# Decoder trunk on one core: attention's third unit turned by a DMA transpose that GpSimd lays out, the second unit's value products placed inside a weight product

## The chip, the cores and the metric

The kernel runs on one core of a Trainium2 chip. The engines are PE (TensorE: matmuls and transposes), DVE (VectorE), ACT (ScalarE), POOL (GpSimd) and SP (SyncE, which here issues DMAs). Each works through its own instructions in order, and semaphores connect them. The metric is the device time of one execution in microseconds (us).

## The reference

The reference is a trunk of two layers on 512 tokens with 1024 features. Each layer is half a gated feed-forward block, a mixer, and a second half feed-forward block:

```
for l in range(DEPTH):                                  # 2
    x = x + 0.5 * swiglu(rms_norm(x, n1), wg1, wu1, wd1)     # D_FF 2816
    h = rms_norm(x, mix_norm[l])
    z = h @ w_in[l]      # q 512 | k 128 | v 128 | conv_B 512 | conv_C 512 | conv_h 512
    attn = sliding_window_attention(q, k, v, attn_sink[l])
    conv = conv_B * depthwise_causal_conv3(conv_C * conv_h)
    x = x + concat([attn, conv]) @ w_out[l]
    x = x + 0.5 * swiglu(rms_norm(x, n2), wg2, wu2, wd2)
return rms_norm(x, final_norm)

# attention: 8 query heads of 64, 2 key/value heads, blocks of 128 tokens,
# each block sees itself and the block before it (window 128)
scores = q @ k_band / 8 + alibi_bias
m = max(max(scores), sink)
p = exp(scores - m) / (sum(exp(scores - m)) + exp(sink - m))
out = p @ v_band
```

All inputs and outputs are float32.

## The kernel before

Matmuls run in a rounded 32-bit format, so every operand is split into a high part (a cast) and a low part (what the cast left). A product of two split operands is three matmuls: high by high, low by high, high by low. Weights are loaded by DMA as `raw`, ACT casts `wh_n` (line 228), DVE subtracts `wl_n` (line 228 too). The number n counts weight slices through the whole program. A slice is split some products ahead of its use: `need_split` issues the split, and `tc.issue_after` pins it behind a given instruction.

The feed-forward blocks use a seven-product scheme (line 842 holds its matmuls). The mixer's input projection `w_in` is worked as 18 slices of 128 output columns. One `product()` of a slice is 24 matmuls over 512 tokens: eight values of k, and for each the three at lines 318 (xh, wh), 319 (xl, wh) and 321 (xh, wl). The first matmul that reads `wl_n` is thus the third of its product.

Attention is cut into eight `Unit(n, g)`, four token blocks by two key/value heads. Units 0 to 3 are the blocks of head group 0, and 4 to 7 those of group 1. In names, `o_0_1_0` is layer 0, block 1, group 0, so unit 1; the third unit is unit 2, `_0_2_0`. A unit has these stages:

- scores: eight matmuls into PSUM tiles `sc` (lines 1554 and 1555). DVE adds the bias and takes maxima, one scan (line 1558, shown as ISA or CUSTOM_DVE_ANT_0) and one accumulator read for each of four heads. It negates the maxima (`nm`, line 1569). ACT takes four exponentials (1575) and that of the sink (`es`, 1578). DVE adds, inverts and scales `p` (1579 to 1583).
- turn: `p` is transposed to have keys on partitions. Units that aren't in `SEND_AT` are turned by PE: per half of the keys four 128x128 transposes into `pt` (1616). ACT then casts `ph` from it (1621), and DVE subtracts `pl` (1622).
- send and join, for the units in `SEND_AT`: ACT copies `p`, as pairs of 16-bit words, into a spare tile `crossing` with the halves of the words apart (1590, 128x2048 u16). SP issues a DMA transpose from there back into `p` (1592). When the unit is to be turned, ACT puts the halves together again (join, 1601, two copies) and `ph` and `pl` come from that.
- values: four matmuls `o` (two for the first block), of `ph` and `pl` with the values `vv` (1633, 1634). ACT copies half of it out (`ol`, 1636), and DVE adds the halves into `mixed[0]` (1639).

The mixer runs in steps. After each `product()` (slices 114 to 125) `go_on()` calls `attend(step)`, from step 6 on. That issues, in this order, the send due at this step, then the values, the turn and the scores of the units whose entries in `VALUES_AT`, `TURN_AT` and `SCORES_AT` are this step. Then `go_on` asks for the next split, pinned behind the last instruction that `attend` returned. The step that is a product's own can put a stage inside it: `INSIDE = (11, 4, 5)` puts unit 4's turn ahead of k = 5 in the product of step 11, which is slice 119. Around the change, step 8 follows product 116, step 9 product 117, step 10 product 118 and step 11 product 119. The order of the code is kept on PE; on DVE and ACT a scheduler orders what the code issues by what it can start when.

Beside attention the same steps run the convolution: DVE multiplies `ch` (1707), ACT makes `cc` and `tap` (1709, 1711), DVE adds the third tap into `tap` (1712), GpSimd adds and multiplies `cc` (1715, 1716).

`mixed` is two tiles of 128x4x512. `mixed[0]` takes attention's output. `mixed[1]` takes the convolution's: columns 0 and 1 after products 118 and 119, columns 2 and 3 after products 124 and 125.

Of the kernel before, what the change touches and what calls it, by code (L numbers as in the profile page):

```python
# [54 lines left out]
STREAM_BACK_AT = {9: 0, 11: 1, 16: 2, 18: 3}  # L55
SCORES_AT = (5, 6, 7, 8, 9, 10, 12, 13)

SEND_AT = {7: 1, 9: 3, 11: 5}
TURN_AT = (6, 9, 8, 11, 10, 13, 14, 15)
VALUES_AT = (7, 10, 9, 12, 11, 14, 15, 16)  # L60
INSIDE = (11, 4, 5)
WARM = 3
XT_TAGS = ("sc", "aux", "aux", "mm", "sc", "sc", "aux", "aux")

# [11 lines left out]
def trunk_kernel(  # L76
# [23 lines left out]
    nc = tc.nc  # L100
# [8 lines left out]
    def psum(tag, shape, name):  # L109
        return ps.tile(shape, F32, tag=tag, bufs={"mm": 4, "sc": 2, "aux": 2}[tag], name=name)  # L110

    def g2(name, dt=F32, shape=(P, S)):
        return work.tile(list(shape), dt, tag="g2", bufs=14, name=name)

    def g8(name, dt=F32R, shape=(P, 2, 2, S)):
        return work.tile(list(shape), dt, tag="g8", bufs=4, name=name)
# [15 lines left out]
    def f32(ap):  # L132
        return ap.bitcast(F32)

    def words(ap):

        return ap.bitcast(U16).rearrange("p (n two) -> p two n", two=2)
# [164 lines left out]
    def take_split(ahead=SPLIT_AHEAD):  # L302
        n = state["group"]
        state["group"] += 1
        need_split(n + ahead)
        return n, *split_of.pop(n)

    def group(rhs, between=None, own=None, order=range(KC), tag="mm"):

        n, hi, lo = own or take_split()  # L310
        acc = psum(tag, [P, S], f"acc_{n}")
        order = order[: len(rhs)]
        first, last = order[0], order[-1]
        late = n == OPEN
        for k in order:
            if between:
                between(k, hi, lo)
            nc.tensor.matmul(acc, hi[:, k, :], rhs[k][0], start=k == first, stop=False)  # L318
            nc.tensor.matmul(acc, hi[:, k, :], rhs[k][1], start=False, stop=False)  # L319
            if not late:  # L320
                nc.tensor.matmul(acc, lo[:, k, :], rhs[k][0], start=False, stop=k == last)  # L321
        if late:
            for k in order:
                nc.tensor.matmul(acc, lo[:, k, :], rhs[k][0], start=False, stop=k == last)
        return acc
# [1168 lines left out]
    def mix(l, norm, after):  # L1494
        q = [None] * NH

        mixed = [g8(f"m_{l}_{j}", F32, (P, KC // 2, S)) for j in range(2)]
# [37 lines left out]
        class Unit:  # L1535
# [49 lines left out]
            def send(self):  # L1585


                self.room = crossing[:, todo.index(self) // 2 % 2, :]
                halves = self.room.bitcast(U16).rearrange("p (two n) -> p two n", two=2)
                nc.scalar.copy(halves, words(self.p.rearrange("p h k -> p (h k)")))  # L1590
                self.turned = self.p.rearrange("p h k -> p (h k)").bitcast(U16)
                nc.sync.dma_start_transpose(
                    self.turned.rearrange("p (c q) -> p c q", q=P),
                    halves.rearrange("p two n -> p (two n)"),
                )
# [11 lines left out]
            def turn(self):  # L1607

                self.pt = []
                for kb in range(self.lo // P, 2):  # L1610
                    if todo.index(self) in SEND_AT.values():
                        tp = self.join(kb)
                    else:
                        tp = psum("aux", [P, 4, P], f"pt_{self.name}_{kb}")
                        for h in range(4):
                            nc.tensor.transpose(
                                tp[:, h, :], self.p[:, h, kb * P : (kb + 1) * P], ident
                            )
                    hi = g2(f"ph_{self.name}_{kb}", F32R, (P, 4, P))
                    lo = g2(f"pl_{self.name}_{kb}", F32R, (P, 4, P))  # L1620
                    nc.scalar.copy(hi, tp)
                    last = nc.vector.tensor_sub(lo, tp, f32(hi))
                    self.pt.append((kb, hi, lo))
                return last

# [17 lines left out]
        todo = [Unit(n, g) for g in range(NKV) for n in range(NT)]  # L1643
        crossing = g8(f"crossing_{l}", F32, (P, 2, 4 * 2 * P))

        def attend(step):

            done = None
            if step in SEND_AT:
                todo[SEND_AT[step]].send()  # L1650
            for at, stage in ((VALUES_AT, "values"), (TURN_AT, "turn"), (SCORES_AT, "scores")):
                if stage == "turn" and step + 1 == INSIDE[0]:
                    done = todo[VALUES_AT.index(step)].added
                    continue
                if step in at:
                    done = getattr(todo[at.index(step)], stage)() or done
            return done

        for j in range(NH // 2):
            acc = group(norm.h) if j else qacc  # L1660
            if j == 3:
                vv = take_values()
            qf = scaled(acc, f"qf_{l}_{j}", by=1.0 / 8.0)
            both = form(f"q_{l}_{j}", shape=(P, 2, S))
            qe, qo = both[:, 0, :], both[:, 1, :]
            nc.scalar.copy(qe[:HD, :], qf[:HD, :])
            nc.scalar.copy(qo[HD:, :], qf[HD:, :])
            nc.vector.tensor_sub(qe[HD:, :], qf[:HD, :], f32(qe[:HD, :]))
            nc.vector.tensor_sub(qo[:HD, :], qf[HD:, :], f32(qo[HD:, :]))
            q[2 * j], q[2 * j + 1] = qe, qo  # L1670
            attend(2 + j)
# [4 lines left out]
        step = 6  # L1676

        def product():

            def between(k, hi, lo):  # L1680
                if step == INSIDE[0] and k == INSIDE[2]:
                    todo[INSIDE[1]].turn()

            return group(norm.h, between, own=take_split(SPLIT_AHEAD - 1))

        def go_on():

            nonlocal step
            last = attend(step)
            if step == TURN_AT[-1]:  # L1690
                state["turned"] = last.ins
            step += 1
            with tc.issue_after(last.ins) if last else nullcontext():
                need_split(state["group"] - 1 + SPLIT_AHEAD + (step >= TURN_AT[-1]))

        for pair in range(2):
            cs = []
            for j in range(2):
                c = g2(f"cc_{l}_{pair}_{j}")
# [4 lines left out]
            for j in range(2):  # L1704
                c = 2 * pair + j
# [13 lines left out]
            for j in range(2):  # L1719
                last = nc.vector.tensor_mul(mixed[1][:, 2 * pair + j, :], product(), ys[j])  # L1720
# [64 lines left out]
```

## Time and profile before

| | |
|---|---|
| time, median of 3 runs | 1626.1 us (1625.88 to 1626.62) |
| profiled execution: its time | 1626.19 us |
| profiled execution: its span | 1624.4 us |
| granted TensorE clock | 0.999 |
| PE busy | 1615.4 us, 99% |
| DVE busy | 1376.7 us, 85% |
| ACT busy | 1178.1 us, 73% |
| POOL busy | 216.5 us, 13% |
| layer 0's attention steps | about 368 to 450 us of the span |
| layer 1's attention steps | about 1171 to 1252 us of the span |

The span runs from the first to the last instruction of the profiled execution; its time holds 1.8 us more. In rows of the timeline the first number is the start in us from the span's start, the second the duration; a suffix x4 says that four like instructions stand in one row. Names there have their numbers left out (`wl` for `wl_119`), so the place in time says which one it is. Matmuls overlap: the start of the next tells more than a duration.

### The profile page before, as it was taken

To read this page: it belongs to the slowest core of one execution; us is meant where nothing else is said; L and a number is where in the kernel's file an instruction comes from. 1 tells how busy PE (TensorE), PEld (TensorE's weight loads), DVE (VectorE), ACT (ScalarE), POOL (GpSimd) and SP (SyncE) were. 2 spreads that over 40 slices of the span, in tenths; PEclk is the share of its full clock that TensorE was granted. 3 is DMA by queue.
4 is the path that set the end of the run, shared out by engine and by line. 5 is a ranking of instruction groups with operands and counts; after the bars stand their busy time and mean duration, and the time that the engine had idled before them with its cause. 6 is when DMAs were issued, how large, how long until landed. Compare 5 with 4: busy or idle time off the path is not lost.

```text
span 1624.4 us, 21158 instructions
## 1 busy us (share of the span) xinstructions
PE 1615.4 (99%) x7571; PEld 1349.4 (83%) x7571; DVE 1376.7 (85%) x1788; ACT 1178.1 (73%) x1511; POOL 216.5 (13%) x191
## 2 busy tenths in 40 slices
PE   9999999999999999999999999999999999999998
PEld 7888888888898888888888888888888988888887
DVE  7978798988899977798998777989688998678997
ACT  6677777857766677778866777788586767878665
POOL 1211111001211111111011111110012111111121
PEclk9999999999999999999999999999999999999999
DMA  9999989822597698999767999998136978999892
GB/s 270 212 232 209 220 207 226 233 59 78 143 227 175 177 225 214 218 214 225 218 144 182 224 215 226 215 221 217 42 91 156 233 149 219 225 223 222 241 230 72
DMA packets 306031, 313.92 MB, mean 193 GB/s; under 512 B 125501, under 2 KB 188549, under 8 KB 305925
## 3 DMA queue, kind: packets, MB, share of 16 engines
q1 hardware_dynamic: 265412, 230.90, 50.1%
q0 software_dynamic: 40048, 81.27, 29.3%
q8 instruction: 59, 0.97, 0.2%
q14 instruction: 48, 0.39, 0.1%
q10 hardware_dynamic: 464, 0.40, 0.1%
HBM read 264.29 MB, written 2.10 MB: 164 GB/s over the span
## 4 chain that ended last, share of the span: by engine, by line
PE 98%; DVE 1%; DMA 0%; SPq 0%; issue 0%; ACT 0%; DVEq 0%
PE x L842 27%; PE y L842 13%; PE x_s L842 9%; PE acc L318 7%; PE acc L319 7%; PE acc L321 7%; PE w L842 7%; PE y_s L842 5%; PE x_m L827 3%; PE w_s L842 3%; PE y_m L827 1%; PE y_e L842 1%; PE acc L699 1%; PE x_e L842 1%; PE w_m L827 1%; PE sc L1555 0%
## 5 line engine op out<-in xcount | busy, mean ns | idle before, releaser
L228 DVE TENSOR_TENSOR wl<-raw,wh 128x1024 fp32r<-128x1024 f32 (+1 forms) x494 | 598.6, 1219 | 162.8 <-ACT wh L228 161.9
L228 ACT CAST wh<-raw 128x1024 fp32r<-128x1024 f32 (+1 forms) x494 | 514.1, 1044 | 304.6 <-PE x L842 92.8
L318 PE MATMUL acc<-xh,wh 128*128 128x512 f32 x392 | 153.3, 393 | 0.5 <-ACT wh L228 0.5
L319 PE MATMUL acc<-xl,wh 128*128 128x512 f32 x392 | 153.1, 391 | 0.0
L321 PE MATMUL acc<-xh,wl 128*128 128x512 f32 x384 | 149.7, 390 | 0.0
L223 POOL DMA_DIRECT2D raw<-in_ffn_wu_dram x40 | 50.6, 1272 | 381.6 <-DMA raw<-in_ffn_wu_dram 268.6
L318 PEld LDWEIGHTS acc<-xh,wh 128*128 128x128 f32 x392 | 73.8, 188 | 15.0 <-ACT wh L228 0.6
L319 PEld LDWEIGHTS acc<-xl,wh 128*128 128x128 f32 x392 | 73.7, 188 | 14.5
L321 PEld LDWEIGHTS acc<-xh,wl 128*128 128x128 f32 x384 | 72.1, 188 | 15.3
L223 POOL DMA_DIRECT2D raw<-in_ffn_wd_dram x34 | 41.0, 1218 | 272.0 <-DMA raw<-in_ffn_wd_dram 122.3
L223 POOL DMA_DIRECT2D raw<-in_ffn_wg_dram x40 | 49.1, 1237 | 201.9 <-DMA raw<-in_ffn_wu_dram 84.7
L269 DVE TENSOR_TENSOR raw<-raw,raw 128x1024 f32<-128x1024 f32 x58 | 70.5, 1220 | 1.7 <-DMA raw<-in_ffn_wu_dram 1.2
L1106 ACT COPY raw_a<-turned 128x1024 uint16<-128x1024 uint16 x48 | 63.5, 1357 | 0.0
L842 PE MATMUL x<-wl,ft1h 128*128 128x512 f32 x160 | 62.4, 390 | 0.0
L842 PE MATMUL w<-wh,fb21h 128*128 128x512 f32 x160 | 62.3, 390 | 0.0
L842 PE MATMUL y<-wh,ft3h 128*128 128x512 f32 x160 | 62.3, 390 | 0.0
L842 PE MATMUL x<-wh,ft1l 128*128 128x512 f32 x160 | 62.3, 389 | 0.0
L842 PE MATMUL x<-wl,ft2h 128*128 128x512 f32 x160 | 62.3, 389 | 0.0
L842 PE MATMUL x<-wh,ft2l 128*128 128x512 f32 x160 | 62.3, 389 | 0.0
L842 PE MATMUL x<-wh,ft1h 128*128 128x512 f32 x160 | 62.3, 389 | 0.0
L842 PE MATMUL w<-wh,fb21l 128*128 128x512 f32 x160 | 62.2, 389 | 0.0
L842 PE MATMUL y<-wh,ft3l 128*128 128x512 f32 x160 | 62.2, 389 | 0.0
(517 smaller groups left out, 4545.2 us busy)
## 6 DMA issues: line engine op xcount, KB each, us to landing
raw<-in_ffn_wu_dram SPq DMA_DIRECT2D x127, 512.0 KB, 5.6
raw<-in_ffn_wd_dram SPq DMA_DIRECT2D x105, 512.0 KB, 5.6
raw<-in_ffn_wg_dram SPq DMA_DIRECT2D x86, 512.0 KB, 5.3
raw<-in_ffn_wu_dram POOLq DMA_DIRECT2D x40, 512.0 KB, 9.1
raw<-in_ffn_wg_dram POOLq DMA_DIRECT2D x40, 512.0 KB, 6.5
raw<-in_w_in_dram SPq DMA_DIRECT2D x36, 512.0 KB, 4.0
raw<-in_ffn_wd_dram POOLq DMA_DIRECT2D x34, 512.0 KB, 8.2
raw<-in_w_out_dram SPq DMA_DIRECT2D x20, 512.0 KB, 4.6
```

The lines of the kernel that those rows point to most:

```text
L223: nc.gpsimd.dma_start(out=r, in_=rows_of(*more), accum_op=ALU.add)
L228: return nc.scalar.copy(hi, raw), eng.tensor_sub(lo, raw, f32(hi))
L269: nc.vector.tensor_add(a11, a11, s1)
L318: nc.tensor.matmul(acc, hi[:, k, :], rhs[k][0], start=k == first, stop=False)
L319: nc.tensor.matmul(acc, hi[:, k, :], rhs[k][1], start=False, stop=False)
L321: nc.tensor.matmul(acc, lo[:, k, :], rhs[k][0], start=False, stop=k == last)
L699: nc.tensor.matmul(opening[n], (lo if part == "w" else hi)[:, k, :], xl if part == "x" else xh, start=n not in begun, stop=k == KC - 1 and ...
L827: nc.tensor.matmul(accs[c // 2][:, c % 2, :], w[:, k, cols], x_[:, 2 * h + k, :], start=start and c % 2 == 0 and h + k + i == 0, stop=h + ...
L842: nc.tensor.matmul(accs[u], x_[:, 2 * h + k, tok], w[:, k, :], start=start and h + k + i == 0, stop=h + k == 2 and i == 2, skip_group_chec ...
L1106: nc.scalar.copy(words(raws[self.b][:, c, :]), self.to[:, :, c, :])
```

## The change

Unit 2 is sent at step 8. GpSimd makes the copy that lays the words apart, and it goes not to `crossing` but to columns 2 and 3 of `mixed[1]`, which are written only after product 124. Unit 2 is turned at step 10 (before: 8) and its values stand at step 11, after product 119 (before: 9, after product 117). Unit 1's values, at step 10 before, now stand inside product 119, ahead of k = 3. Unit 4's turn stays inside that product ahead of k = 5. What the next split is pinned to at step 10 is the last subtraction `pl` of unit 1 (`parted`), where it was the last addition into `mixed[0]`.

```diff
-SEND_AT = {7: 1, 9: 3, 11: 5}
-TURN_AT = (6, 9, 8, 11, 10, 13, 14, 15)
-VALUES_AT = (7, 10, 9, 12, 11, 14, 15, 16)
-INSIDE = (11, 4, 5)
+SEND_AT = {7: 1, 8: 2, 9: 3, 11: 5}
+TURN_AT = (6, 9, 10, 11, 10, 13, 14, 15)
+VALUES_AT = (7, None, 11, 12, 11, 14, 15, 16)
+INSIDE = {(11, 3): (1, "values"), (11, 5): (4, "turn")}
+IDLE_LAYS = (2,)
...
             def send(self):
-                self.room = crossing[:, todo.index(self) // 2 % 2, :]
+                n = todo.index(self)
+                self.room = crossing[:, n // 2 % 2, :]
+                if n == 2:
+                    self.room = mixed[1][:, 2:4, :].rearrange("p c s -> p (c s)")
                 halves = self.room.bitcast(U16).rearrange("p (two n) -> p two n", two=2)
-                nc.scalar.copy(halves, words(self.p.rearrange("p h k -> p (h k)")))
+                whole = words(self.p.rearrange("p h k -> p (h k)"))
+                (nc.gpsimd.tensor_copy if n in IDLE_LAYS else nc.scalar.copy)(halves, whole)
...
-                    last = nc.vector.tensor_sub(lo, tp, f32(hi))
+                    last = self.parted = nc.vector.tensor_sub(lo, tp, f32(hi))
...
             for at, stage in ((VALUES_AT, "values"), (TURN_AT, "turn"), (SCORES_AT, "scores")):
-                if stage == "turn" and step + 1 == INSIDE[0]:
-                    done = todo[VALUES_AT.index(step)].added
-                    continue
-                if step in at:
-                    done = getattr(todo[at.index(step)], stage)() or done
+                for n in (n for n, when in enumerate(at) if when == step):
+                    if (n, stage) in INSIDE.values():
+                        done = todo[1].parted
+                    else:
+                        done = getattr(todo[n], stage)() or done
...
             def between(k, hi, lo):
-                if step == INSIDE[0] and k == INSIDE[2]:
-                    todo[INSIDE[1]].turn()
+                if (step, k) in INSIDE:
+                    n, stage = INSIDE[step, k]
+                    getattr(todo[n], stage)()
```

In the rows of order that follow, numbers behind the last underscore only tell tiles apart, and lines of the changed kernel are one to six higher. All rows are layer 0's; layer 1 has the same.

PE, from the end of product 118 (`acc_118`) into product 119, before: unit 1's four value matmuls, unit 5's eight score matmuls (`sc_0_1_1`), then the product.

```order
L321 MATMUL acc_118_3575<-xh_1_6_2840,wl_118_3480 128x512
L1633 MATMUL o_0_1_0_3601<-ph_0_1_0_0_3528,vv_0_3202 128x512
L1634 MATMUL o_0_1_0_3601<-pl_0_1_0_0_3529,vv_0_3202 128x512
L1633 MATMUL o_0_1_0_3601<-ph_0_1_0_1_3533,vv_0_3202 128x512
L1634 MATMUL o_0_1_0_3601<-pl_0_1_0_1_3534,vv_0_3202 128x512
L1554 MATMUL sc_0_1_1_0_3612<-kh_0_3070,q_0_2_3159 128x256
...
L1555 MATMUL sc_0_1_1_1_3619<-kl_0_3071,q_0_3_3207 128x256
L318 MATMUL acc_119_3648<-xh_1_0_2886,wh_119_3571 128x512
L319 MATMUL acc_119_3648<-xl_1_0_2887,wh_119_3571 128x512
L321 MATMUL acc_119_3648<-xh_1_0_2886,wl_119_3572 128x512
```

The same place in the changed kernel:

```order
L322 MATMUL acc_118_3550<-xh_1_6_2840,wl_118_3464 128x512
L1555 MATMUL sc_0_1_1_0_3588<-kh_0_3070,q_0_2_3159 128x256
...
L319 MATMUL acc_119_3624<-xh_1_0_2886,wh_119_3546 128x512
L320 MATMUL acc_119_3624<-xl_1_0_2887,wh_119_3546 128x512
L322 MATMUL acc_119_3624<-xh_1_0_2886,wl_119_3547 128x512
...
L322 MATMUL acc_119_3624<-xh_1_2_2932,wl_119_3547 128x512
L1638 MATMUL o_0_1_0_3634<-ph_0_1_0_0_3503,vv_0_3202 128x512
L1639 MATMUL o_0_1_0_3634<-pl_0_1_0_0_3504,vv_0_3202 128x512
L1638 MATMUL o_0_1_0_3634<-ph_0_1_0_1_3508,vv_0_3202 128x512
L1639 MATMUL o_0_1_0_3634<-pl_0_1_0_1_3509,vv_0_3202 128x512
L319 MATMUL acc_119_3624<-xh_1_2_2932,wh_119_3546 128x512
```

Unit 1's values moved from ahead of product 119 to behind its ninth matmul, so the first reader of `wl_119` comes earlier in PE's row. The eight transposes `pt_0_2_0` inside product 117 are gone, and unit 2's four values moved from behind product 117 to behind product 119.

DVE, around the maxima of units 2 and 3 (`nm_0_2_0`, `nm_0_3_0`), before:

```order
L1558 ISA mx_0_2_0_3356 128x1
L1569 TENSOR_SCALAR nm_0_2_0_3372<-mx_0_2_0_3356 128x4
L1571 TENSOR_TENSOR es_0_2_0_3374<-sink_78,nm_0_2_0_3372 128x4
L1579 TENSOR_TENSOR sums_0_2_0_3376<-sums_0_2_0_3376,es_0_2_0_3374 128x4
L1707 TENSOR_TENSOR ch_0_0_0_3394<-acc_116_3395,cc_0_0_0_3246 128x512
...
L1712 SCALAR_TENSOR_TENSOR tap_0_0_3422<-ch_0_0_0_3394,par_88,tap_0_0_3422 128x510
L1622 TENSOR_TENSOR pl_0_2_0_0_3433<-pt_0_2_0_0_3427,ph_0_2_0_0_3432 128x512
L1622 TENSOR_TENSOR pl_0_2_0_1_3442<-pt_0_2_0_1_3436,ph_0_2_0_1_3441 128x512
L1569 TENSOR_SCALAR nm_0_3_0_3461<-mx_0_3_0_3445 128x4
L228 TENSOR_TENSOR wl_118_3480<-raw_90_3126,wh_118_3479 128x1024
```

And in the changed kernel:

```order
L1559 ISA mx_0_2_0_3356 128x1
L229 TENSOR_TENSOR wl_118_3464<-raw_90_3126,wh_118_3463 128x1024
L1570 TENSOR_SCALAR nm_0_2_0_3372<-mx_0_2_0_3356 128x4
L1572 TENSOR_TENSOR es_0_2_0_3374<-sink_78,nm_0_2_0_3372 128x4
...
L1584 TENSOR_SCALAR p_0_2_0_3357<-p_0_2_0_3357,sums_0_2_0_3376 128x256 x4
L1718 SCALAR_TENSOR_TENSOR tap_0_0_3422<-ch_0_0_0_3394,par_88,tap_0_0_3422 128x510
L1559 ISA p_0_3_0_3430,mx_0_3_0_3429<-sc_0_3_0_1_3438,bias_356,sink_78 128x256
L1559 ISA mx_0_3_0_3429 128x1
L1570 TENSOR_SCALAR nm_0_3_0_3445<-mx_0_3_0_3429 128x4
L1572 TENSOR_TENSOR es_0_3_0_3447<-sink_78,nm_0_3_0_3445 128x4
```

`wl_118` moved from behind `nm_0_3_0` to ahead of `nm_0_2_0`. The two `pl_0_2_0` left this place, and the scaling of unit 2's `p` now directly precedes `tap_0_0`. On GpSimd the new copy, `COPY m_0_1_2959<-p_0_2_0_3357 128x2048`, stands right ahead of the first operations on `cc_0_0_0`.

ACT, from unit 3's exponentials to unit 4's (`p_0_0_1`), before:

```order
L1575 ACTIVATE p_0_3_0_3446,sums_0_3_0_3465<-p_0_3_0_3446,nm_0_3_0_3461 128x256 x4
L1578 ACTIVATE es_0_3_0_3463<-es_0_3_0_3463 128x4
L1709 ACTIVATE cc_0_0_1_3320<-ch_0_0_1_3483,par_88 128x512
L1711 ACTIVATE tap_0_1_3511<-ch_0_0_1_3483,par_88 128x511
L1636 COPY ol_0_2_0_3523<-o_0_2_0_3518 64x512
L1621 CAST ph_0_1_0_0_3528<-crossing_0_3080 128x512
L1590 COPY crossing_0_3080<-p_0_3_0_3446 128x2048
L1621 CAST ph_0_1_0_1_3533<-crossing_0_3080 128x512
L228 CAST wh_120_3644<-raw_92_3314 128x1024
L228 CAST wh_121_3704<-raw_93_3388 128x1024
L1575 ACTIVATE p_0_0_1_3538,sums_0_0_1_3557<-p_0_0_1_3538,nm_0_0_1_3553 128x128 x4
```

And in the changed kernel, from one row earlier:

```order
L229 CAST wh_119_3546<-raw_91_3164 128x1024
L1576 ACTIVATE p_0_3_0_3430,sums_0_3_0_3449<-p_0_3_0_3430,nm_0_3_0_3445 128x256 x4
L1579 ACTIVATE es_0_3_0_3447<-es_0_3_0_3447 128x4
L229 CAST wh_120_3620<-raw_92_3314 128x1024
L1715 ACTIVATE cc_0_0_1_3320<-ch_0_0_1_3467,par_88 128x512
L1717 ACTIVATE tap_0_1_3495<-ch_0_0_1_3467,par_88 128x511
L1595 COPY crossing_0_3080<-p_0_3_0_3430 128x2048
L1626 CAST ph_0_1_0_0_3503<-crossing_0_3080 128x512
L1576 ACTIVATE p_0_0_1_3513,sums_0_0_1_3532<-p_0_0_1_3513,nm_0_0_1_3528 128x128
L1626 CAST ph_0_1_0_1_3508<-crossing_0_3080 128x512
L1576 ACTIVATE p_0_0_1_3513,sums_0_0_1_3532<-p_0_0_1_3513,nm_0_0_1_3528 128x128 x3
L1579 ACTIVATE es_0_0_1_3530<-es_0_0_1_3530 128x4
```

The two casts `wh_119` and `wh_120` stand next to unit 3's exponentials. The send of unit 3 (`crossing_0_3080<-p_0_3_0`) moved ahead of both casts `ph_0_1_0`, and unit 4's exponentials begin between these. On DVE, `pl_0_1_0_0` and `pl_0_1_0_1`, which had six other instructions between them, now stand together behind unit 4's `nm_0_0_1` and `es_0_0_1`, and `wl_119` follows them directly. On SP, unit 2's DMA transpose stands ahead of unit 3's, and the load of `raw_95` moved behind both.

## The prediction

> **What bounds the kernel now.** I read the page's busy shares and chain first, then PE's waits, then the timelines of the four engines at the place the change touches.
>
> ```profile
> span 1624.4 us, 21158 instructions
> PE 1615.4 (99%) x7571; PEld 1349.4 (83%) x7571; DVE 1376.7 (85%) x1788; ACT 1178.1 (73%) x1511; POOL 216.5 (13%) x191
> PE 98%; DVE 1%; DMA 0%; SPq 0%; issue 0%; ACT 0%; DVEq 0%
> ```
>
> The third row is the chain that ended last: it is PE almost throughout. PE's waits by releaser say the same:
>
> ```profile
> PE idle L151 <- DVE warm L646: 1.2, 1, 1.2
> PE xt L665 <- DMA xin<-in_x_dram: 0.6, 1, 0.6
> PE acc L318 <- ACT wh L228: 0.5, 1, 0.5
> ```
>
> These 2.3 us are all the idle time that the profile records on PE. So only two things can move the time: matmuls that PE no longer does, and new waits of PE. A busy DVE or ACT is free until a product of PE comes to weights that aren't split yet. All times below are layer 0's in the profiled execution; layer 1 runs the same order, so each term counts twice.
>
> **What PE saves.** PE's timeline, first at the removed transposes, then at the second unit's values and the product after them:
>
> ```profile
> 389.81 1.12 PE L1616 MATMUL pt<-ident,p 128*128 128x128 f32 x8
> 391.01 0.39 PE L321 MATMUL acc<-xh,wl 128*128 128x512 f32 x1
> ...
> 402.62 0.39 PE L1633 MATMUL o<-ph,vv 128*128 128x512 f32 x1
> 403.08 0.39 PE L1633 MATMUL o<-ph,vv 128*128 128x512 f32 x1
> 403.43 0.50 PE L1634 MATMUL o<-pl,vv 128*128 128x512 f32 x1
> 403.76 0.28 PE L1554 MATMUL sc<-kh,q 128*128 128x256 f32 x1
> 404.71 0.40 PE L318 MATMUL acc<-xh,wh 128*128 128x512 f32 x1
> 405.19 0.39 PE L321 MATMUL acc<-xh,wl 128*128 128x512 f32 x1
> ```
>
> Matmuls overlap, so I count from start to start. A 512-column matmul takes 0.23 (two from 402.62 to 403.08). From the first transpose to the L321 at 391.01 lie eight transposes and one matmul: 1.20 less 0.23 leaves 0.97 saved. The four value matmuls of the second unit (o, 402.62 to 403.76) take 1.14, where four without a wait take 0.92: they lose 0.22 to pl, 0.11 of it in the restart (the late one shows 0.50 against 0.39). Moved into product 119, their pl is earlier in the row than wl_119 on DVE, which PE has by then, so that wait goes as well. Saved: 0.97 + 0.22 = 1.19 per layer. The eight values' matmuls that only change place (units 1 and 2) cost PE what they did.
>
> But they come later, and so product 119 comes earlier. Its first reader of wl_119 is the L321 at 405.19. Ahead of it are now missing the transposes (0.97), the third unit's values (four at 0.23, 0.92) and the second unit's (1.14): it is due at 405.19 - 3.03 = 402.16.
>
> **What the weights of product 119 now stand behind.** DVE's timeline:
>
> ```profile
> 385.50 0.17 DVE L1569 TENSOR_SCALAR nm<-mx 128x4 f32<-128x4 f32 x1
> 389.19 1.13 DVE L1583 TENSOR_SCALAR p<-p,sums 128x256 f32<-128x256 f32 x4
> 391.48 0.75 DVE L1712 SCALAR_TENSOR_TENSOR tap<-ch,par,tap 128x510 f32<-128x510 f32 x1 [0.34 <-ACT tap L1711]
> 394.40 0.66 DVE L1569 TENSOR_SCALAR nm<-mx 128x4 f32<-128x4 f32 x1
> 394.98 1.21 DVE L228 TENSOR_TENSOR wl<-raw,wh 128x1024 fp32r<-128x1024 f32 x1
> 396.11 0.15 DVE L1571 TENSOR_TENSOR es<-sink,nm 128x4 f32<-128x4 f32 x1
> 400.48 1.18 DVE L1622 TENSOR_TENSOR pl<-crossing,ph 128x512 fp32r<-128x512 f32 x1
> 402.40 0.97 DVE L1622 TENSOR_TENSOR pl<-crossing,ph 128x512 fp32r<-128x512 f32 x1
> 403.37 1.21 DVE L228 TENSOR_TENSOR wl<-raw,wh 128x1024 fp32r<-128x1024 f32 x1
> ```
>
> In the last row wl_119 ends at 404.58, 0.61 ahead of its reader. That is all the slack there was, against 3.03 of advance; even with DVE as before there would be a wait. And DVE is later. First, wl_118 (394.98 to 396.11, 1.13) now stands ahead of the third unit's nm at 385.50. The exponentials, and the scale at 389.19, come 1.1 later: by the new row the scale ends near 391.35. Then GpSimd may copy the third unit.
>
> GpSimd and DVE have been in each other's way in this stage already:
>
> ```profile
> 393.74 1.29 POOL L1716 TENSOR_TENSOR cc<-cc,inv 128x512 f32<-128x512 f32 x1
> 401.19 1.63 POOL L1716 TENSOR_TENSOR cc<-cc,inv 128x512 f32<-128x512 f32 x1
> ```
>
> The nm of 394.40 took 0.66 where the one of 385.50 took 0.17; it ends at 395.06, just behind GpSimd's 393.74 + 1.29 = 395.03. The pl at 402.40 ends at 403.37 in place of 403.09, and GpSimd's operation at 401.19 has 1.63 in place of 1.29. So a scaling by DVE within SBUF, and a subtraction with both inputs there, wait for a GpSimd operation to end, and the other way round. In the changed order the tap operation (0.67 to the next) follows the scale at once, to 392.02, and the copy waits for it: it runs from 392.0 to 392.0 + X. One scan and one accumulator read follow on DVE (0.40), so the fourth unit's nm is due at 392.45, inside the copy: it ends 0.05 behind it, at 392.05 + X. It is the twin of the row at 394.40.
>
> [...]
>
> **Size of X.** No row has GpSimd copying u16. The nearest, from GpSimd's groups with shapes kept apart (the mean in ns stands behind the busy time):
>
> ```profile
> L173 POOL CAST ones_r<-ones 128x128 fp32r<-128x128 f32 x1 | 0.3, 288 | 0.0
> L1772 POOL MEMSET const-float32-0.0<- 128x1 f32 x1 | 0.1, 99 | 0.2 <-issue 0.2
> ```
>
> A cast has one input as the copy has: 288 less the 99 of a one-element operation over 128 elements is 1.48 ns each; times 2048, plus 0.1, gives 3.1. Upper end: the two-input row, 1.29 less 0.10 over 512, 2.3 ns each, 4.9. Lower end: ACT does this same copy in 1.90 (below). I take 3.1, since it is the one-input row of that engine.
>
> **From nm to wl_119.** ACT's timeline has each operation that stands between them:
>
> ```profile
> 395.10 0.51 ACT L1575 ACTIVATE p<-p,nm 128x256 f32<-128x256 f32 x1 [1.33 <-DVE nm L1569]
> 397.18 0.71 ACT L1709 ACTIVATE cc<-ch,par 128x512 f32<-128x512 f32 x1
> 397.79 0.71 ACT L1711 ACTIVATE tap<-ch,par 128x511 f32<-128x511 f32 x1
> 398.52 0.59 ACT L1636 COPY ol<-o 64x512 f32<-64x512 f32 x1
> 399.53 1.90 ACT L1590 COPY crossing<-p 128x2048 uint16<-128x2048 uint16 x1
> 401.33 0.62 ACT L1621 CAST ph<-crossing 128x512 fp32r<-128x512 f32 x1
> 401.85 1.99 ACT L228 CAST wh<-raw 128x1024 fp32r<-128x1024 f32 x2
> 403.75 0.40 ACT L1575 ACTIVATE p<-p,nm 128x128 f32<-128x128 f32 x1
> ```
>
> In the new order ACT does, after nm: four exponentials and es (395.10 to 397.18, 2.08), wh_120 (half of 401.85 to 403.75, 0.95), cc (0.61), tap (0.73), the fourth unit's send (1.80), ph (0.52), one exponential (0.40), the second ph (0.62): 7.71. DVE then does the second pl (0.61) and wl_119 (1.22). GpSimd's two operations on cc follow the tap, as before, and hold the two pl: 1.18 + 0.97 less twice 0.69 is 0.77. Some 0.08 goes for hand-overs. So wl_119 ends at 392.05 + X + 7.71 + 1.83 + 0.77 + 0.08 = 402.44 + X, and PE, due at 402.16, waits X + 0.28.
>
> What else goes or moves: the third unit's two hi casts from PSUM become casts from its crossing, its two joins add 2.7 to ACT, and its values stand behind product 119. With the same durations ACT ends its second ph near 406.3 + X, and PE, released at 402.4 + X with 22 matmuls, four values and four transposes ahead (6.5), comes near 408.9 + X: covered by 2, and if not, a wait of the excess. The transfer on SP takes, by the view of the tile crossing (median us to landing, last):
>
> ```profile
> p<-crossing SPq DMA_TRANSPOSE x6, 3.7
> ```
>
> It lands near 396 + X, the join starts near 401 + X: hidden. SP's next weight load stands behind it, later by its issue (1.6) and by its slot; with that load's split five products ahead I cost it at nothing.
>
> Per layer: X + 0.28 - 1.19 + 0.11 for a restart = X - 0.80; with X = 3.1, 2.3. Twice, 4.6. The profiled execution took 1626.19 with a span of 1624.4; with the 1.8 around it unchanged that is 1630.8. The median of the runs is 0.09 below it, so **1630.7**.
>
> The bounds: X = 1.9 gives 2.2 more, 1628.3; X = 4.9 gives 8.2 more, 1634.3.
>
> **Rivals.** 0.2% (3.25 us) is about what a measurement of this kernel can tell from no change.
>
> *A short copy, or one that DVE isn't held by.* At X = 1.9 the time is 1628.3; without a hold nm is out near 392.6, but ACT isn't free then: from es on, 1.1 later than in the first row below (its timeline) and so ended at 389.0, it has cc and tap (1.34), two joins (second row, of the tile crossing: min, median and max in ns; 2.72) and wh_119 (0.95) to do, until 394.0. That is as if X were 1.95, or 1628.4.
>
> ```profile
> 387.69 0.19 ACT L1578 ACTIVATE es<-es 128x4 f32<-128x4 f32 x1
> ...
> L1601 ACT COPY crossing<-p x12: 1339/1359/1373, 388.9 to 1223.0; 128x1024 uint16<-128x1024 uint16 x12
> ```
>
> For it: the one ACT row; against: the twin at 394.40. It decides below X = 2.45, where twice X - 0.80 is 3.25 or less. [...] Chance 0.20.
>
> *A long copy.* The two-input row's pace or more, because every other u16 word is taken: 1634.3 and up. Against it: the copy has one input. Chance 0.15.
>
> *No wait at all: the saving alone.* If wl_119 is ready by 402.16, the time is 1626.1 - 2 x 1.19 = 1623.7, which is not slower, and within 0.2%. It needs DVE to take wl_119 (wh_119 is cast by 394.0) ahead of the two pl; the new row has them the other way round, so ACT's 7.71 would have to be nearly free. The point that decides is 402.16. Chance 0.10.
>
> **Chances.** The forecast, X between 2.45 and 4.2, has 0.55. Slower: 0.55 + 0.15 = 0.70. Within 0.2%: most of 0.20 and 0.10, 0.26. Faster by over 0.2%: 0.04, for a gain that I don't see; all that PE saves is 0.15%. The range 1627.0 to 1635.3 takes in both bounds of X with an us to spare and leaves out the saving alone and a still longer copy.
>
> **What the profile after would show.** A POOL copy of 128x2048 near 392, of about 3.1; an nm right at its end; a wait of PE on wl, L321's successor, of some 3.4 in each layer, ended by DVE; no wait of PE on pl; the transposes 16 fewer. I am wrong if PE shows no wait there, if the copy overlaps an undisturbed nm, or if PE's wait is on another operation than wl_119.

## The result

The changed kernel takes 1630.04 us, the median of 10 runs (1629.45 to 1631.30), against 1626.26 us before (10 runs, 1625.78 to 1626.75). The ratio is 1.0025, with a 95% interval of 1.0015 to 1.0034: slower by a quarter of a per cent. The profiled execution took 1630.18 us, with a span of 1628.4.

Two rows of the changed kernel's page, and from PE's waits the row that the change concerns (us in total, times, longest; line numbers are one to six higher than before):

```profile
span 1628.4 us, 21137 instructions
PE 1614.9 (99%) x7555; PEld 1348.1 (83%) x7555; DVE 1383.9 (85%) x1788; ACT 1182.9 (73%) x1515; POOL 220.1 (14%) x193
...
PE acc L322 <- DVE wl L229: 3.7, 2, 1.9
```

The 16 transposes are gone. In their place PE waits for `wl_119` in layer 0 and for its twin in layer 1, 1.9 us each time. This is layer 0 on PE:

```profile
401.89 0.40 PE L320 MATMUL acc<-xl,wh 128*128 128x512 f32 x1
404.16 0.50 PE L322 MATMUL acc<-xh,wl 128*128 128x512 f32 x1 [1.87 <-DVE wl L229]
404.50 0.40 PE L319 MATMUL acc<-xh,wh 128*128 128x512 f32 x1
...
405.89 0.39 PE L1638 MATMUL o<-ph,vv 128*128 128x512 f32 x1
...
406.81 0.39 PE L319 MATMUL acc<-xh,wh 128*128 128x512 f32 x1
```

The reader of `wl_119` would have been due 0.23 after 401.89, at 402.12. It starts at 404.16, which is 2.04 lost, and 0.11 more go in the restart (404.16 to 404.50 in place of 0.23). The second unit's four values now take 0.92 (405.89 to 406.81) and wait for nothing.

GpSimd and DVE at the place that the prediction is about:

```profile
391.33 2.26 POOL L1595 COPY m<-p 128x2048 uint16<-128x2048 uint16 x1 [45.29 <-DVE p L1584]
393.56 1.28 POOL L1721 TENSOR_TENSOR cc<-cc,tap 128x511 f32<-128x511 f32 x1
```

```profile
391.11 0.74 DVE L1718 SCALAR_TENSOR_TENSOR tap<-ch,par,tap 128x510 f32<-128x510 f32 x1
...
392.28 1.34 DVE L1570 TENSOR_SCALAR nm<-mx 128x4 f32<-128x4 f32 x1
...
399.30 1.16 DVE L1570 TENSOR_SCALAR nm<-mx 128x4 f32<-128x4 f32 x1
...
400.57 2.40 DVE L1627 TENSOR_TENSOR pl<-crossing,ph 128x512 fp32r<-128x512 f32 x2
402.89 1.21 DVE L229 TENSOR_TENSOR wl<-raw,wh 128x1024 fp32r<-128x1024 f32 x1
```

The `nm` of the fourth unit (unit 3) is issued at 392.28 and ends at 393.62, right behind the copy (391.33 + 2.26 = 393.59), where such an operation alone takes 0.17. `wl_119` ends at 404.10.

PE's own starts, compared matmul by matmul with those of before, are 0.04 earlier at the start of layer 0's attention, 0.95 later at that of layer 1's, and 3.93 later at the last matmul. Layer 0 costs 1.0 and layer 1 costs 3.0, although the same wait stands in both. The difference is in the rows behind the wait in layer 1:

```profile
1207.90 0.50 PE L322 MATMUL acc<-xh,wl 128*128 128x512 f32 x1 [1.87 <-DVE wl L229]
...
1208.93 0.57 PE L319 MATMUL acc<-xh,wh 128*128 128x512 f32 x1
1209.30 0.63 PE L320 MATMUL acc<-xl,wh 128*128 128x512 f32 x1
1209.72 0.63 PE L322 MATMUL acc<-xh,wl 128*128 128x512 f32 x1
...
1212.28 0.45 PE L320 MATMUL acc<-xl,wh 128*128 128x512 f32 x1
...
1212.80 0.39 PE L319 MATMUL acc<-xh,wh 128*128 128x512 f32 x1
```

The same in windows of that stretch, where the third number from the end (ahead of the DMA's share and GB/s) is the granted clock:

```profile
1205.00:1208.00 3.00, 1.13 (x8) 0.70 (x6) 3.00 (x5) 3.00 (x10) 0.56 (x1) 1.00 0.69 156
1209.00:1210.00 1.00, 1.00 (x4) 0.81 (x3) 1.00 (x3) 1.00 (x3) 0.00 (x0) 0.50 0.65 182
1212.00:1213.00 1.00, 1.00 (x5) 0.81 (x4) 1.00 (x6) 1.00 (x3) 0.00 (x0) 0.80 1.04 312
```

About 1.1 us after PE resumed, its granted clock fell to 0.50, and it came back some 3.4 us later. Ten matmuls took 3.87 (1208.93 to 1212.80) in place of 2.28, so this cost 1.6 us. Over the whole span it shows as a mean clock of 0.998 in place of 0.999. Of the ten runs two have 0.997, at 1631.27 and 1631.30; seven have 0.998, six of them with 1629.45 to 1630.21 and one with 1631.29; one has 1.0, at 1629.71. That time, no lower than the others, this doesn't explain.

### The profile page after: what moved, and what is told of

The parts are those of the page before. It is cut to its first block, busy times and chain, and to the rows that moved or that the text cites. A ratio compares the mean times of both kernels' runs of the same rounds, so it can differ in the third digit from the quotient of the medians.

```text
span 1628.4 us, 21137 instructions
## 1 busy us (share of the span) xinstructions
PE 1614.9 (99%) x7555; PEld 1348.1 (83%) x7555; DVE 1383.9 (85%) x1788; ACT 1182.9 (73%) x1515; POOL 220.1 (14%) x193
## 4 chain that ended last, share of the span: by engine, by line
PE 96%; DVE 3%; ACT 1%; DMA 0%; issue 0%; SPq 0%; DVEq 0%
PE x L843 27%; PE y L843 13%; PE x_s L843 9%; PE acc L319 7%; PE acc L320 7%; PE w L843 7%; PE acc L322 7%; PE y_s L843 5%; PE x_m L828 3%; PE w_s L843 3%; PE y_m L828 1%; PE y_e L843 1%; PE acc L700 1%; PE x_e L843 1%; PE w_m L828 1%; DVE wl L229 0%
## 5 line engine op out<-in xcount | busy, mean ns | idle before, releaser
L322 PE MATMUL acc<-xh,wl 128*128 128x512 f32 x384 | 150.1, 391 | 3.7 <-DVE wl L229 3.7
L322 PEld LDWEIGHTS acc<-xh,wl 128*128 128x128 f32 x384 | 72.3, 188 | 19.9 <-DVE wl L229 4.6
L843 PE MATMUL x<-wh,ft2h 128*128 128x512 f32 x160 | 62.3, 389 | 0.0
```

Source lines behind the costliest of these rows:

```text
L843: nc.tensor.matmul(accs[u], x_[:, 2 * h + k, tok], w[:, k, :], start=start and h + k + i == 0, stop=h + k == 2 and i == 2, skip_group_chec ...
```

## The experiments

Each kernel was timed in turns with the kernel before on the same chip (medians of before: 1626.42 beside e1, e3, e4 and e5; 1626.15 beside e7, e8, e2 and e9; 1626.33 beside e6, e11 and e12).

| kernel | median us | ratio to before, 95% |
|---|---|---|
| changed kernel | 1630.04 | 1.0025 (1.0015 to 1.0034) |
| e1_free_split | 1632.03 | 1.0039 (1.0027 to 1.0052) |
| e3_values_only | 1628.74 | 1.0013 (1.0005 to 1.0022) |
| e4_dma_only | 1628.79 | 1.0015 (1.0006 to 1.0024) |
| e5_kept_busy | 1633.34 | 1.0037 (1.0024 to 1.0051) |
| e7_no_conv_ops | 1628.04 | 1.0012 (1.0003 to 1.0021) |
| e8_half_copy | 1631.07 | 1.0030 (1.0018 to 1.0041) |
| e2_act_copy | 1629.07 | 1.0018 (1.0009 to 1.0027) |
| e9_half_busy | 1629.81 | 1.0022 (1.0013 to 1.0031) |
| e6_copy_twice | 1633.98 | 1.0045 (1.0032 to 1.0059) |
| e11_join_less | 1629.08 | 1.0016 (1.0007 to 1.0026) |
| e12_again (the changed kernel) | 1630.91 | 1.0025 (1.0015 to 1.0035) |

Medians that differ by less than 1 us shouldn't be ranked. The intervals are wider than that, and at the program's start, away from the change, PE waits for its first input for 0.2 us in all in e4's profile and for 2.0 in e3's.

Two theories stood against each other. By the first, which is the prediction's, GpSimd's copy holds `nm`, and everything up to `wl_119` follows from there. By the second, the copy is beside the point: ACT's load or GpSimd's convolution operations make `wl_119` late, or the order that puts it behind the two `pl`.

### The split of slice 119 set free

```diff
-            with tc.issue_after(last.ins) if last else nullcontext():
+            with tc.issue_after(last.ins) if last and step != 10 else nullcontext():
                 need_split(...)
```

> The changed kernel, but the split of slice 119 is no longer pinned behind the second unit's last pl (the instruction order puts wl_119 right behind unit 3's nm and es instead). If the whole loss is PE's wait for wl_119, which ended at 404.10 in layer 0 and 1207.84 in layer 1, that wait is gone and the 1.2 us that PE saves per layer stay: 1623.8 to 1624.6. If the loss comes from elsewhere (the transfers, a later stage), it stays at 1628 or above.

The wait for `wl_119` is indeed gone: PE's L322 of product 119 runs 3 us ahead of before (402.26 against 405.19). But the time is 1632.03, more than the changed kernel's. PE now waits in each layer at the fifth unit's values:

```profile
413.96 0.50 PE L1638 MATMUL o<-ph,vv 128*128 128x512 f32 x1 [2.98 <-ACT ph L1626]
```

```profile
413.11 0.19 ACT L1579 ACTIVATE es<-es 128x4 f32<-128x4 f32 x1
413.32 0.58 ACT L1626 CAST ph<-pt 128x512 fp32r<-128x512 f32 x1
```

The second fence is ACT's: it casts this `ph` at 413.32, since the new order puts it behind the next unit's four exponentials and their `es`. What PE saved was lost a product later to ACT, and more. The expected 1623.8 missed that: it took the stage to have one late operation, and the next ones are late too.

### Each half of the change alone

Values only (the third unit turned by PE as before):

```diff
-SEND_AT = {7: 1, 8: 2, 9: 3, 11: 5}
-TURN_AT = (6, 9, 10, 11, 10, 13, 14, 15)
-VALUES_AT = (7, None, 11, 12, 11, 14, 15, 16)
+SEND_AT = {7: 1, 9: 3, 11: 5}
+TURN_AT = (6, 9, 8, 11, 10, 13, 14, 15)
+VALUES_AT = (7, None, 9, 12, 11, 14, 15, 16)
```

> Only the second unit's values moved inside product 119; the third unit is turned by PE as before. The reader of wl_119 is due 1.14 earlier, at 404.05, and wl_119 ends as before at 404.58: a wait of some 0.6 with 0.11 for the restart, less the 0.22 that the values no longer lose, is 0.5 per layer: 1627.2. If placing the values inside a product costs nothing by itself: 1625.8 or below.

```profile
405.16 0.50 PE L322 MATMUL acc<-xh,wl 128*128 128x512 f32 x1 [0.44 <-DVE wl L229]
412.40 0.50 PE L1638 MATMUL o<-ph,vv 128*128 128x512 f32 x1 [0.47 <-ACT ph L1626]
```

The first row is the wait that was expected (0.62 from the time it was due, and 0.10). The second was not: 0.64 and 0.11 more at the fifth unit's `ph`. The time is 2.3 over before where 1.1 was expected. In the profiled execution (1629.10) 0.5 lies ahead of layer 0's attention, away from the change, and the layers cost 1.1 and 1.3.

The DMA transpose only (the second unit's values ahead of product 119 as before):

```diff
-VALUES_AT = (7, None, 11, 12, 11, 14, 15, 16)
-INSIDE = {(11, 3): (1, "values"), (11, 5): (4, "turn")}
+VALUES_AT = (7, 10, 11, 12, 11, 14, 15, 16)
+INSIDE = {(11, 5): (4, "turn")}
...
-                        done = todo[1].parted
+                        done = todo[1].added
```

> Only the third unit's turn by DMA transpose with GpSimd's copy; the second unit's values stand ahead of product 119 as before. DVE's order up to wl_119 is that of the changed kernel. PE comes to the second unit's values at 400.7 and waits there for pl (302.9 on the changed kernel's DVE means 402.9) instead of for wl_119, with the values done by then: 0.4 per layer over before, 1627.0, and no wait of 2 us in one piece. If the copy by GpSimd is what the change loses by: 1628.3 or above.

(The 302.9 in it is a slip for 402.9.)

```profile
402.39 0.50 PE L1639 MATMUL o<-pl,vv 128*128 128x512 f32 x1 [1.31 <-DVE pl L1627]
```

The wait has moved from `wl_119` to `pl`, as expected, and is shorter. Small waits at the third and fourth units' `pl` (0.12 to 0.26, and 0.11 for each restart) bring the layer to 1.0 over before, not 0.4. The time lies in the range that the expectation gave to the copy; but this run can't tell the copy from the other late work, since DVE's order up to `wl_119` is that of the changed kernel. Each half alone thus costs about as much per layer as both together, 1.0 to 1.3 without half clock: the costs don't add. Both run into the same late operations, `ph` of ACT and `pl` and `wl` of DVE.

### What holds DVE: the convolution on GpSimd

```diff
-                nc.gpsimd.tensor_add(y[:, 1:], y[:, 1:], tap[:, 1:])
-                nc.gpsimd.tensor_mul(y, y, norm.inv)
+                if c != 1:
+                    nc.gpsimd.tensor_add(y[:, 1:], y[:, 1:], tap[:, 1:])
+                    nc.gpsimd.tensor_mul(y, y, norm.inv)
```

> The changed kernel without GpSimd's two operations on the convolution's second column (cc_0_0_1 in layer 0, its twin in layer 1), which are left out; the order of all other instructions is the same. In the changed kernel unit 4's nm (399.30, 1.16) and the two pl (400.57, 2.40) are drawn out beside these operations. If they decide when wl_119 is ready, it ends about 1.1 earlier, at 403.0 in layer 0, and PE loses 0.9 in place of 2.0 at its reader. If the copy of the third unit decides, wl_119 ends at 404.1 as before.

```profile
402.25 0.40 PE L320 MATMUL acc<-xl,wh 128*128 128x512 f32 x1
403.49 0.50 PE L322 MATMUL acc<-xh,wl 128*128 128x512 f32 x1 [0.84 <-DVE wl L229]
```

```profile
399.66 0.17 DVE L1570 TENSOR_SCALAR nm<-mx 128x4 f32<-128x4 f32 x1
...
400.70 0.69 DVE L1627 TENSOR_TENSOR pl<-crossing,ph 128x512 fp32r<-128x512 f32 x1 [0.68 <-ACT ph L1626]
401.61 0.69 DVE L1627 TENSOR_TENSOR pl<-crossing,ph 128x512 fp32r<-128x512 f32 x1 [0.21 <-ACT ph L1626]
```

PE loses 1.01 (403.49 less 402.48) in place of 2.04, and the drawn-out `nm` and `pl` are back at 0.17 and 0.69. So 1.0 of the 2.0 is due to these two GpSimd operations. The layer gains less, 0.2 to 0.3 by PE's starts, because waits at the third and fourth units' `pl` grow to 0.36 and 0.45.

### The copy: half, twice, and by ACT

```diff
-                (nc.gpsimd.tensor_copy if n in IDLE_LAYS else nc.scalar.copy)(halves, whole)
+                if n in IDLE_LAYS:
+                    nc.gpsimd.tensor_copy(halves[:, :, :512], whole[:, :, :512])
+                else:
+                    nc.scalar.copy(halves, whole)
...
+        nc.gpsimd.memset(mixed[1][:, 2:4, :], 0.0)
```

> The changed kernel with GpSimd copying only half of the third unit's words (the other half of the tile is zeroed early in the layer, so that half of the turned unit is zero); the order of DVE, ACT and PE is the same. If the fourth unit's nm, held until the copy ends, sets wl_119 (the sum of the prediction), each us off the copy is a us off PE's wait: 0.9 less per layer. If ACT, which works until 393.55 in layer 0 while the copy ends at 393.59, is as late by itself, wl_119 ends at most 0.15 earlier.

```profile
391.13 1.03 POOL L1596 COPY m<-p 128x1024 uint16<-128x1024 uint16 x1 [44.75 <-DVE p L1584]
393.05 1.29 POOL L1725 TENSOR_TENSOR cc<-cc,tap 128x511 f32<-128x511 f32 x1 [0.89 <-DVE tap L1722]
```

```profile
390.36 1.94 DVE L1584 TENSOR_SCALAR p<-p,sums 128x256 f32<-128x256 f32 x4
392.23 0.74 DVE L1722 SCALAR_TENSOR_TENSOR tap<-ch,par,tap 128x510 f32<-128x510 f32 x1
...
393.41 0.96 DVE L1570 TENSOR_SCALAR nm<-mx 128x4 f32<-128x4 f32 x1
```

This did not tell the theories apart. The half copy needs only two heads, so it started between the four scalings and drew them out to 1.94, where the four took 1.13 before (389.19). `nm` came late and was caught by the next GpSimd operation, until 394.37. PE lost 2.27 at `wl_119`. What it did give is a price: 1.03 for 1024 words.

```diff
                 (nc.gpsimd.tensor_copy if n in IDLE_LAYS else nc.scalar.copy)(halves, whole)
+                if n in IDLE_LAYS:
+                    nc.gpsimd.tensor_copy(halves, whole)
```

> The changed kernel with GpSimd's copy of the third unit made twice in a row; the order of DVE, ACT and PE is the same. The second copy shows GpSimd's time for these words without DVE's tap ahead of it; by the half copy (1.03 for 1024) it is 1.9, not the 3.1 that the prediction took. By the prediction's sum (unit 4's nm ends with the copy, 10.4 from there to the end of wl_119) wl_119 ends later by that time, and PE loses 3.9 in place of 2.0 in each layer: 1632.1 without a stretch of half clock, up to 1636 with two. If the copy doesn't stand on the path, PE's loss stays 2.0.

```profile
391.02 2.27 POOL L1595 COPY m<-p 128x2048 uint16<-128x2048 uint16 x1 [45.29 <-DVE p L1584]
393.25 1.28 POOL L1723 TENSOR_TENSOR cc<-cc,tap 128x511 f32<-128x511 f32 x1
394.47 1.89 POOL L1597 COPY m<-p 128x2048 uint16<-128x2048 uint16 x1
```

(The "unit 4's nm" of the expectation is the fourth unit's, unit 3's.) The second copy takes 1.89: that is X. It was placed behind the first convolution operation, not behind the first copy, so `nm` was not held by it (it ended at 393.31, behind the first). PE lost 3.1 in place of 2.0, from holds further on, not the 3.9 expected. PE's clock stood at half for 14 matmuls in layer 0 and 8 in layer 1, and that is how the time comes to lie between the 1632.1 and the 1636 of the expectation.

```diff
-IDLE_LAYS = (2,)
+IDLE_LAYS = ()
```

> The changed kernel with the third unit's words laid apart by ACT, as those of the other sent units, in place of GpSimd. If GpSimd's copy and its hold on DVE are what the change loses by, the time falls to 1626.2 or below. If ACT and DVE are the bound of this stage, ACT's 1.8 more takes the place of the hold and the time stays within 0.5 per layer of the changed kernel's: 1628.3 to 1631.

```profile
401.96 0.40 PE L320 MATMUL acc<-xl,wh 128*128 128x512 f32 x1
403.76 0.50 PE L322 MATMUL acc<-xh,wl 128*128 128x512 f32 x1 [1.41 <-DVE wl L229]
```

```profile
392.35 1.02 DVE L1570 TENSOR_SCALAR nm<-mx 128x4 f32<-128x4 f32 x1
392.54 1.92 ACT L1595 COPY m<-p 128x2048 uint16<-128x2048 uint16 x1
```

1629.07 is inside the second range. With the copy on ACT, PE still loses 1.57 at `wl_119` (403.76, due at 402.19; 1.60 in layer 1) and 0.45 at the fourth unit's `ph`: the change does not lose by the choice of GpSimd. But this run does not free `nm` either: GpSimd's convolution operation (392.05, 1.29) now holds it until 393.37, and ACT, with the copy, comes to the exponentials only at 394.33.

### ACT relieved

```diff
             def join(self, kb):
                 whole = self.room[:, kb * 4 * P : (kb + 1) * 4 * P]
+                if todo.index(self) == 1 and kb == 1:
+                    return whole.rearrange("p (h q) -> p h q", h=4)
```

> The changed kernel without the second of the two copies by which ACT joins the second unit's words (left out, so that half of that unit is wrong); ACT's and DVE's order is otherwise the same but for one scan. ACT is done with wh_119 1.2 earlier, at 392.3 in layer 0, and waits for the fourth unit's nm. If nm, held behind GpSimd until 393.6, is what the rest follows, wl_119 ends at most 0.3 earlier and PE loses 1.7 to 2.0. If ACT's load decides, it ends up to 1.2 earlier and PE loses 0.8.

```profile
393.85 0.51 ACT L1576 ACTIVATE p<-p,nm 128x256 f32<-128x256 f32 x1 [1.33 <-DVE nm L1570]
404.15 0.50 PE L322 MATMUL acc<-xh,wl 128*128 128x512 f32 x1 [1.67 <-DVE wl L229]
```

The same place on ACT in the changed kernel:

```profile
392.48 1.07 ACT L229 CAST wh<-raw 128x1024 fp32r<-128x1024 f32 x1
393.66 0.51 ACT L1576 ACTIVATE p<-p,nm 128x256 f32<-128x256 f32 x1
```

In e11 ACT idles 1.33 ahead of the fourth unit's exponentials, and waits for `nm`, which the copy holds until 393.81. `wl_119` ends at 404.09, as in the changed kernel, and PE loses 1.84 (404.15, due at 402.31). So at this point the hold decides, as the prediction had it. But in the changed kernel ACT itself was done only at 393.55, 0.1 before it got `nm`: by these rows either alone would have made it about as late. No run takes the hold on `nm` away and leaves the rest, so that isn't shown.

### The half clock

> The changed kernel with eight more 512-column matmuls at the start of product 119 in each layer (they write what the product's first matmul then overwrites), 1.84 us of work in the place of the wait for wl_119. PE's wait shrinks to about 0.2. If the wait alone is the loss, nothing changes: 1630.0 as measured for the changed kernel. If the half clock that follows the wait in layer 1 (1209.0 to 1212.4) is brought on by PE's idleness, there is no such stretch and the time is 1628.3, before's 1626.2 and 1.05 for each layer.

```diff
+            state["acc"] = acc
...
+                if step == 11 and k == 0:
+                    for _ in range(8):
+                        nc.tensor.matmul(state["acc"], hi[:, 0, :], norm.h[0][0], start=True, stop=True)
```

This did not give the answer. The added matmuls changed the order behind product 119 (ACT's cast of the fifth unit's `ph` went behind exponentials), PE waited there for 1.10 and 0.38 us, and the time rose to 1633.34. Half clock came all the same in layer 1, right behind those two waits.

> The changed kernel with four more 512-column matmuls at the start of product 119 in each layer, 0.9 us of work that the product's first matmul overwrites. wl_119 is ready when it was, so the path is as long; only PE's wait in one piece falls from 2.0 to 1.1. If the stretches of half clock come from that idleness, the granted clock is before's 0.999 and the time 1628.3; if not, 1630.0 with a clock of 0.998 or 0.997 as in the ten runs of the changed kernel.

With four of them (`range(4)`) PE loses 1.11 in one piece, in both layers, and the profile has no half clock:

```profile
404.18 0.50 PE L323 MATMUL acc<-xh,wl 128*128 128x512 f32 x1 [0.95 <-DVE wl L229]
```

The granted clock is on record for every run. In the profiles a stretch of half clock lowers its mean over the span by about 0.001: it is 0.999 or 1.0 without one, 0.998 with one and 0.997 with two (e12; 0.996 in e6, where one of the two lasts 6.8 us). Here all 11 runs have 0.999 or 1.0, where 16 of the 18 runs of the changed kernel (the ten and e12's eight) have 0.998 or 0.997. So the clock did what the first half of the expectation says: with a shorter idle piece, and `wl_119` as late, the half clock is gone.

The time did not follow. The profiled execution took 1629.04, but the median of the runs is 1629.81, only 0.2 below the changed kernel's, where 1.7 was expected. In the profile the layers cost 1.3 and 1.5 rather than 1.0, from other small waits; what the other runs lost isn't shown.

> The changed kernel once more, for a second profile. PE's wait for wl_119 is 2.0 in each layer again, and wl_119 ends at 404.1. If the half clock after that wait falls by chance on one layer or the other, the profile has it in other places than the first (layer 1, from 1209.0), and its time is 1628.3 and 1.9 for each such stretch.

```profile
385.00:425.00 40.00, 38.13 (x178) 31.65 (x177) 35.16 (x97) 35.18 (x67) 7.41 (x5) 0.96 0.47 119
1185.00:1230.00 45.00, 43.12 (x204) 35.88 (x203) 40.10 (x111) 38.74 (x71) 7.43 (x5) 0.96 0.46 118
```

The same program, the same two waits of 1.87, and this time half clock behind both (0.96 in both windows, where the first profile had 1.00 and 0.96): 1631.41. With two stretches 1632.1 was expected; 1631.41 less 1628.3 is 3.1, 1.6 for each, as counted above, and not 1.9. The lowest of its eight runs, 1628.66, is the only one with a clock of 0.999: by that it had no such stretch, and it is near the 1628.3.

Over all profiles: in the four with a loss of 2.0 to 3.1 at `wl_119` (the changed kernel twice, e6, e8) half clock follows in 6 of 8 layers. In the six whose longest loss is 0.6 to 1.8 (e2, e3, e4, e7, e9, e11) it follows in none of 12, and none of the 63 runs of these six has a clock below 0.999. The step is sharp: e11, with 1.84, has it in none of 10 runs, and e12, beside it on the same chip, with 2.04, in 7 of 8. In e6's layer 0 the clock fell while PE still waited, as this window shows (no matmul, clock 0.50):

```profile
404.30:404.90 0.60, 0.00 (x0) 0.00 (x0) 0.60 (x3) 0.60 (x2) 0.00 (x0) 0.50 0.00 0
```

Two kernels stand aside. e1 waits 2.98 at another place and has no half clock in its profile, though two of its five runs have clocks of 0.998 and 0.996. e5, with two waits close together, has it in 1 of 2 layers. So at this place the half clock goes with PE's idleness: none of 11 runs has it at a loss of 1.11 (e9) and none of 10 at 1.84 (e11), but 16 of 18 have it at 2.04 (the changed kernel). Why e1's longer waits bring it on less often, and what decides between the layers, stays open.

## Why the prediction was right, and where it was not

The time (1630.04 against 1630.7) lies in the range, and the direction is right, by the wait that was forecast. That the number came so close is luck: X made the sum about 2.4 us too long (1.2 in each layer), and the half clock, which the sum did not have, put 1.6 on in the profiled execution.

- **What PE saves** held: transposes 0.97 (PE is 1.00 ahead behind them), the second unit's wait gone, and the reader of `wl_119` due at 402.12 against 402.16.
- **The hold** came as forecast: `nm` ended 0.03 behind the copy, as its twin did before, and ACT relieved of a join gains nothing by it. `nm` shows 1.34, where the one at 385.50 before took 0.17, and the copy, behind DVE's tap, shows 2.26, where the second one of e6 takes 1.89.
- **X failed.** The term "the size of X" took 3.1 from the cast's row. That row is 128 elements long. At the pace of the copies (1.89 less 1.03 over 1024 words, 0.84 ns each) they take 0.11 of its 0.29, so by this estimate 0.18 was fixed and not 0.10, and the difference was multiplied by 16. The copy takes 1.89, the lower bound, ACT's time for the same words. It could also start about 0.3 earlier than in the sum, since DVE was through with the tap operation ahead of it at 391.76 and not at 392.02. `nm` ended at 393.62 and not at 395.15, and PE lost 2.04 and not 3.4.
- **From `nm` to `wl_119`** held as a sum: 10.48 (393.62 to 404.10) against 10.39. A part was undersized: GpSimd's convolution operations, 0.77 in the sum, which had them on the two `pl` alone, gave back 1.0 when taken away. They hold unit 4's `nm` too (1.16 in place of 0.17).
- **The covers** held: the transfer, SP's load and the third unit's `ph` (ended at 407.48, PE there at 410.67) cost nothing. The fourth unit's `pl` was not thought of, and costs 0.29 and 0.11 in layer 0.
- **The half clock was not foreseen.** The sum had PE resume at full speed. In the profiled execution it cost 1.6 in one layer, in the repeat it came in both. This term the sum put at nothing.

So by mechanism the rival "a short copy" is what happened. It was given 0.20 and 1628.3; without half clock the measured lengthening would be about 4.0 less 1.6, 2.4 on the profiled execution, 1628.6. What moved it to 1630 is a cost that no case had. The rival "no wait at all" was not tried in a clean form: freeing the split took the wait away, and the next one, at the fifth unit's `ph`, was longer (2.98). That is the larger lesson about this stage. Here is a window of 27 us, before and then after; the columns are its length, the busy time of PE, PEld, DVE, ACT and POOL, the clock, the DMA share and GB/s:

```profile
386.00:413.00 27.00, 27.00 (x137) 22.39 (x136) 23.10 (x72) 25.20 (x58) 5.51 (x4) 1.00 0.43 115
```

```profile
386.00:413.00 27.00, 25.13 (x125) 20.84 (x124) 24.16 (x67) 25.92 (x57) 7.40 (x5) 1.00 0.53 137
```

ACT was busy for 25.2 of them before, and for 25.9 after; DVE went from 23.1 to 24.2. PE's saving of 1.2 could only be had if ACT and DVE delivered as much earlier, and they had little left to give. In every variant some wait appeared, at `wl`, `pl` or `ph`.

## What to carry to other kernels

Work taken from a bound engine in one stage, as here, is a gain only if the engines that feed it there have slack (ACT was busy for 25.9 of 27 us here): read their busy time in that window, not over the span, before counting the saving. A price scaled up from an operation a sixteenth as long scales up its fixed cost too (0.18 of 0.29 here, by the estimate above), so keep the range to the nearest long operation, even on another engine. A wait of PE of 2.04 us cost 1.6 more than its length in layer 1 here: look for matmuls of 0.63 in place of 0.39 behind it.

## What the runs showed of the hardware that was not expected

- After waits that cost PE 2.0 to 3.1 us its granted clock fell to 0.50 in 6 of 8 cases. In the five of them that the changed kernel, e6 and e12 show, it began between 0.6 ahead of PE's resuming and 1.1 us after it, and lasted 3.4 us, and in e6 once 6.8 (404.3 to 411.1). The stretch that was counted cost 1.6 us. Where the loss was 1.84 (e11) none of 10 runs had it, and where it was 1.11 (e9) none of 11.
- GpSimd copies 2048 u16 words, every other one taken, in 1.89 us (1024 in 1.03), as fast as ACT does (1.88 to 1.92).
- GpSimd's hold on DVE can be passed on: with the shorter copy, or with none, `nm` fell behind the next GpSimd operation instead (0.96, ended 394.37; 1.02, ended 393.37).
